# Gate and input of a short convolution: weights stationary in quarters of 256 channels, or activations stationary in halves of 512 channels with a transposed product

## The chip, the cores and the metric

The kernel runs on one core of one Trainium2 chip. The metric is the device time in microseconds (us); the median of three runs is given. A core has five engines that run beside each other: TensorE (PE in the profile; its weight loads are PEld), VectorE (DVE), ScalarE (ACT), GpSimd (POOL) and SyncE (SP), which issues most of the loads here.

## The reference

A trunk of two layers (D_MODEL 2048, SEQ 256, float32). Every layer has attention and a short gated convolution side by side, and behind them an MLP:

```python
h = _rmsnorm(x, attn_norm_g[l])
proj = h @ w_in[l]
q, k, v, gate_b, gate_c, conv_in = jnp.split(proj, splits, axis=-1)    # 1024 columns each
...                                # differential attention, 8 heads -> attn (256 x 1024)
conv = gate_b * _short_conv(gate_c * conv_in, conv_w[l])
x = x + jnp.concatenate([attn, conv.astype(attn.dtype)], axis=-1) @ w_out[l]
hm = _rmsnorm(x, mlp_norm_g[l]) @ w_up[l]
x = x + jnp.square(jax.nn.relu(hm)) @ w_down[l]

def _short_conv(u, w):             # causal, depthwise, CONV_K = 3
    S = u.shape[1]
    up = jnp.pad(u, ((0, 0), (CONV_K - 1, 0), (0, 0)))
    return sum(w[i] * up[:, i:i + S] for i in range(CONV_K))
```

## The kernel before

Every float32 operand of a matrix product is split in two parts: `hi`, a ScalarE copy into a shorter format (L341, tile `whi` for weights), and `lo`, the rest, a VectorE subtraction (L342, `wlo`). A product is the sum of three: hi by hi, hi by lo, lo by hi (`TERMS`). TensorE runs in the order in which the program is written. The other engines are ordered by a tile scheduler.

Two things decide that written order. One is the list of weight jobs: loads of weights into `raw` buffers (four), and their splits (three buffers of each part). They are made in the order of the list, three ahead of the use (`take`). The other is background work: generators (attention of a head, normalisation and so on) that are moved on one piece each time the program calls `work.tick()`, with a number of ticks to wait between pieces. So a head's scores (L712 on), its transposes (`ptp`, L747; `atp`, L793) and its products stand between the matmuls of a projection.

The mixer of one layer goes so: q and k by a scheme that replaces eight block products by seven (`BySeven`); v in two halves of 512 columns by `linear` (L441 to L461: activations are stationary, the weights move as 512 columns, and the result lies by token); then **the stretch that the change rewrites**, with attention in the background; then **the stage of the gate columns**; then the right half of W_out, and the MLP.

The stretch that is rewritten has four quarters of 256 channels. Each has gate_C (`gc`) and conv_in (`ci`), made by `linear_t` (L463 to L488): here 128x128 blocks of weights are stationary and the activations move, hi and lo parts together as 512 columns for `whi`, the hi part alone as 256 columns for `wlo` (both L481). The result lies by channel and has two halves that `joined` adds (ScalarE copy, L493, and VectorE sum, L495: tiles `gc03l`, `gc03w` and the like, the first figure the layer and the second the quarter). The input h is not normalised yet in these products. The factor 1/rms of each token is brought in as a row over all partitions (`norm.bc`): its square multiplies `gc` on GpSimd, and the row itself multiplies the convolved product on GpSimd. The product u = ci * gc is on VectorE, tap 2 of the convolution on ScalarE and taps 1 and 0 on VectorE (L815), all in SBUF.

The stage of the gate columns (`left`) takes its steps from a list, `LEFT`. A step makes a column of 128 gate_B channels (`gb`, by `column_part`, L433, with the same 512 and 256 columns), multiplies it with the convolved product `cv` (`gate`, L824 to L828), or runs products of the seven-product scheme (`po`, L941) on weight splits `w7b`, `w7t`, `w7x` (L880, L916 to L921). `banks` opens the PSUM accumulators of these products. PSUM has two double tiles for accumulators (`mm2`), three single banks used in turn (`bank`) and one for attention (`av`).

Of the kernel before, what the change touches and what calls it, by code (L numbers as in the profile page):

```python
# [133 lines left out]
def trunk(ctx: ExitStack, tc: tile.TileContext, x, w_in, w_out, conv_w, q_norm_g, k_norm_g,  # L134
# [191 lines left out]
    class Weights:  # L326
# [94 lines left out]

        def turned(self, w, col):
            for i in range(D // P // 4):
                self.plain(w, 4 * P * i, col, 4)

    def column_part(acc, acts, weights):
# [13 lines left out]

    def linear(name, acts, weights):  # L441

        acc = mm.tile([P, NT, CH], F32, tag="mm2", name=name)
        nk = len(acts) * KG
        for kp in range(nk // 2):
            hi, lo = weights.take()
            for j in range(2):
                k = kp * 2 + j
                a = acts[k // KG]
                while not a.ready:  # L450
                    work.tick()
                steps = [(t, pa, pw) for t in range(NT) for pa, pw in TERMS]
                if weights.ramp and weights.used == 1 and j == 0:
                    steps = [(t, pa, pw) for pa, pw in ((0, 0), (1, 0), (0, 1)) for t in range(NT)]
                for t, pa, pw in steps:
                    nc.tensor.matmul(  # L456
                        acc[:, t], a.ap[:, pa, k % KG, t * P:(t + 1) * P], (hi, lo)[pw][:, j],
                        start=(k == 0 and (pa, pw) == (0, 0)),
                        stop=(k == nk - 1 and (pa, pw) == TERMS[-1]))
                work.tick()  # L460
        return acc  # L461

    def linear_t(name, acts, weights):  # L463

        acc = mm.tile([P, 2, 2, S], F32, tag="mm2", name=name)
        nk = len(acts) * KG
        for k0 in range(0, nk, 8):  # L470

            tiles = [weights.take() for _ in range(2)]
            for part in range(2):
                for k in range(k0, k0 + 8):
                    a = acts[k // KG]
                    while not a.ready:
                        work.tick()
                    wt = tiles[(k - k0) // 4][part]
                    for f in range(2):
                        fs = slice(f * P, (f + 1) * P)  # L480
                        nc.tensor.matmul(  # L481
                            acc[:, f, 0] if part else acc[:, f], wt[:, k % 4, fs],
                            a.ap[:, 0, k % KG] if part else a.ap[:, :, k % KG],
                            start=(part == 0 and k == 0), stop=(part == 1 and k == nk - 1),
                            skip_group_check=True)
                    if k % 4 == 3 or (part == 0 and k % 2 == 0):
                        work.tick()
        return acc  # L488

    def joined(acc, name):  # L490

        low = nat.tile([P, 2, S], F32, tag="wide", name=f"{name}l")
        nc.scalar.activation(low, acc[:, :, 1], AF.Copy)  # L493
        whole = nat.tile([P, 2, S], F32, tag="wide", name=f"{name}w")
        nc.vector.tensor_add(whole, acc[:, :, 0], low)  # L495
        return whole

# [8 lines left out]
    class Norm:  # L506
# [71 lines left out]
        def factors(self):  # L578
# [25 lines left out]
            while held:  # L604
# [3 lines left out]
                             start=True, stop=True)  # L608
            self.across = small.tile([P, 2, S], F32, tag="rowb", name="rowb", bufs=1)
            nc.vector.tensor_copy(self.across[:, 0], tp[:, :S])  # L610
            nc.gpsimd.tensor_tensor(self.across[:, 1], self.across[:, 0], self.across[:, 0],
                                    op=ALU.mult)

        def bc(self, power):

            return self.across[:, power - 1].unsqueeze(1).to_broadcast([P, 2, S])

# [74 lines left out]
    def attention(l, qT, kT, kL, v, h0, dst, bias, tmp, pace, sums_of):  # L692
# [4 lines left out]
        OFF = (0, P)  # L697
        r0 = small.tile([P, 4, NT], F32, tag="r0", name=f"r0_{h0}", bufs=2)
        ss = small.tile([P, 4, NT], F32, tag="ams", name=f"ams{h0}", bufs=2)
        ao = tmp.tile([P, NT, CH], F32, tag="ao", name=f"ao{h0}", bufs=1)  # L700

        def unit(i):
# [28 lines left out]
            for t in range(NT):  # L731
                for m in range(2):
                    e = s[:, m, OFF[t]:OFF[t] + (t + 1) * P]
                    nc.scalar.activation(e, e, AF.Exp, bias=nm[:, t, m:m + 1],
                                         accum_out=su[:, t, m:m + 1])
            rc = small.tile([P, NT, 2], F32, tag="rc", name=f"rc{h}")
            nc.vector.reciprocal(rc, su)
            nc.vector.tensor_copy(r0[:, i], rc[:, :, 0])
            c = small.tile([P, NT], F32, tag="c", name=f"c{h}", bufs=3)
            p = s[:, 0]  # L740
            for t in range(NT):
                w = slice(OFF[t], OFF[t] + (t + 1) * P)
                nc.vector.scalar_tensor_tensor(c[:, t:t + 1], su[:, t, 0:1], rc[:, t, 1:2],
                                               nlam[:, l:l + 1], op0=ALU.mult, op1=ALU.mult)
                nc.vector.scalar_tensor_tensor(p[:, w], s[:, 1, w], c[:, t:t + 1], s[:, 0, w],
# [27 lines left out]
            flat = ss.rearrange("p i t -> p (i t)")  # L773
            rflat = r0.rearrange("p i t -> p (i t)")
            for _ in range(2):
# [32 lines left out]

    def conv(l, q, u, cv, norm):

        for i in range(2):
            k = q * 2 + i
            nc.scalar.activation(cv[:, k], u[:, i], AF.Copy, scale=tap(l, 2, k))
            for back in (1, 2):
                nc.vector.scalar_tensor_tensor(  # L815
                    cv[:, k, back:], u[:, i, :S - back], tap(l, 2 - back, k),
                    cv[:, k, back:], op0=ALU.mult, op1=ALU.add)
        pair = cv[:, q * 2:q * 2 + 2]
        nc.gpsimd.tensor_tensor(pair, pair, norm.bc(1), op=ALU.mult)

# [15 lines left out]
    class BySeven:  # L836
# [160 lines left out]

        def left(self, acts, cv):

# [174 lines left out]
    def mixer(l, norm, loads):  # L1174

        with ExitStack() as scope:
# [66 lines left out]
            cv = bpool.tile([P, AW // P, S], F32, tag="b", name=f"cv{l}")  # L1243
            for q in range(AW // WC):
# [9 lines left out]
            by_seven.left(hT, cv)  # L1254
            mnorm = Norm(1, l)
# [497 lines left out]
```

## Time and profile before

| | |
|---|---|
| time, median of three runs | 2112.55 us (2112.5 to 2112.66) |
| span of the profiled execution (its own time is given by this span alone) | 2110.7 us |
| median less span | 1.85 us |
| granted TensorE clock | 1.000 |
| TensorE busy (of which it loads weights) | 2105.2 us, 100% (1799.0 us, 85%) |
| VectorE, ScalarE, GpSimd busy | 1834.6 us 87%, 1407.5 us 67%, 189.4 us 9% |
| moved by DMA | 476.01 MB, mean 226 GB/s |

Busy times are sums of one engine's instructions; engines overlap, so they don't add up to the span. A row of the timeline has the start in us from the span's start, the duration of the run of like instructions, engine, line, operation, and out<-in with the tile names (buffer numbers left out), shape and count. Matmuls are pipelined: each lasts longer than the distance to the next one's start, so distances between starts are what adds up. In the table of windows each row is a stretch A:B, its length, then the busy time and count of TensorE, TensorE's weight loads, VectorE, ScalarE and GpSimd, the clock, the share of DMA and its GB/s; with a line named, the times are those of that line's instructions alone. In the timeline, a bracket at a row's end is idle time of the engine ahead of it and what ended it.

### The profile page before, as it was taken

What the parts mean: (1) busy time and instruction counts of PE and PEld (TensorE: products, weight loads), DVE (VectorE), ACT (ScalarE), POOL (GpSimd) and SP (SyncE); (2) the same over time, 40 slices, a digit from 0 to 9 for tenths busy, and PEclk for the clock granted to TensorE, in tenths of its full rate; (3) what the DMA queues carried; (4) which work ended last, traced back from release to release, by engine and by line L of the source; (5) the groups of instructions that cost most, each with busy time, mean ns of one, the idle gap of its engine ahead of it and who ended that gap; (6) DMA issues with size and microseconds to landing.
All of it is one profiled execution on the core that took longest, in us unless ns stands there. A gap on an engine that the chain in (4) does not pass through costs nothing.

```text
span 2110.7 us, 29252 instructions
## 1 busy us (share of the span) xinstructions
PE 2105.2 (100%) x10809; PEld 1799.0 (85%) x10809; DVE 1834.6 (87%) x2525; ACT 1407.5 (67%) x1823; POOL 189.4 (9%) x226
## 2 busy tenths in 40 slices
PE   9999999999999999999999999999999999999999
PEld 7888888888888888888888888888888888888887
DVE  7888788898888888799888887988988888888998
ACT  6777566676776766666566775657676677675664
POOL 2211120000000000011101121000000000000110
PEclk9999999999999999999999999999999999999999
DMA  7655575887777777789566456668777777777993
GB/s 265 205 154 167 171 216 182 289 259 229 230 238 229 231 232 230 251 291 310 171 220 188 152 170 185 195 193 290 255 238 229 229 230 238 230 229 260 315 309 113
DMA packets 312607, 476.01 MB, mean 226 GB/s; under 512 B 12723, under 2 KB 209669, under 8 KB 312464
## 3 DMA queue, kind: packets, MB, share of 16 engines
q1 hardware_dynamic: 284752, 406.76, 60.7%
q0 software_dynamic: 27520, 67.24, 10.1%
q8 instruction: 85, 1.39, 0.3%
q14 instruction: 58, 0.48, 0.1%
q10 hardware_dynamic: 192, 0.15, 0.0%
HBM read 440.52 MB, written 33.58 MB: 225 GB/s over the span
## 4 chain that ended last, share of the span: by engine, by line
PE 98%; DMA 1%; POOL 1%; DVE 1%; issue 0%; ACT 0%; ACTq 0%; DVEq 0%
PE upc L1427 31%; PE pr L1470 14%; PE dn L1551 8%; PE gc L481 4%; PE ci L481 4%; PE gb L433 4%; PE v L456 3%; PE q L958 3%; PE o L958 3%; PE k L958 3%; PE dn L1470 3%; PE po L941 2%; PE dn L1645 2%; PE pr1r L1470 2%; PE pr0r L1470 2%; PE po L958 2%
## 5 line engine op out<-in xcount | busy, mean ns | idle before, releaser
L1427 PE MATMUL upc<-nT,uhi 128*128 128x512 f32 x1920 | 454.7, 389 | 0.0
L1427 PEld LDWEIGHTS upc<-nT,uhi 128*128 128x128 f32 x1920 | 360.2, 188 | 74.7
L1292 DVE TENSOR_TENSOR ulo<-uraw,uhi 128x1024 fp32r<-128x1024 f32 x256 | 312.3, 1222 | 109.8 <-ACT f L1459 91.5
L341 ACT ACTIVATE whi<-raw 128x1024 fp32r<-128x1024 f32 x232 | 244.7, 1058 | 180.2 <-issue 21.8
L1291 ACT ACTIVATE uhi<-uraw 128x1024 fp32r<-128x1024 f32 x256 | 270.6, 1057 | 135.7 <-PE upc L1427 115.4
L342 DVE TENSOR_TENSOR wlo<-raw,whi 128x1024 fp32r<-128x1024 f32 x232 | 284.3, 1234 | 53.1 <-ACT whi L341 46.9
L1427 PEld LDWEIGHTS upc<-nT,ulo 128*128 128x128 f32 x1920 | 246.2, 191 | 9.4
L1427 PE MATMUL upc<-nT,ulo 128*128 128x256 f32 x1920 | 249.1, 283 | 0.0
L1317 ACT ACTIVATE bh<-draw 128x1536 fp32r<-128x1536 f32 x86 | 128.3, 1492 | 103.7 <-PE pr L1470 82.1
L1318 DVE TENSOR_TENSOR bl<-draw,bh 128x1536 fp32r<-128x1536 f32 x86 | 151.3, 1759 | 11.4 <-ACT bh L1317 10.9
L1551 PE MATMUL dn<-whi,fb 128*128 128x512 f32 x480 | 152.0, 389 | 0.0
L1470 PE MATMUL pr<-bh,f 128*128 128x512 f32 x360 | 121.4, 391 | 0.0
L341 ACT ACTIVATE whi<-uraw 128x1024 fp32r<-128x1024 f32 x60 | 63.7, 1062 | 72.0 <-PE dn L1551 58.5
L1437 ACT ACTIVATE ev<-upc 128x512 f32<-128x512 f32 x120 | 72.0, 600 | 54.0 <-PE upc L1427 54.0
L1317 ACT ACTIVATE t24h<-t 128x1024 fp32r<-128x1024 f32 x86 | 91.4, 1063 | 23.7 <-PE pr L1470 15.9
L1551 PEld LDWEIGHTS dn<-whi,fb 128*128 128x128 f32 x480 | 90.1, 188 | 18.6
L1318 DVE TENSOR_TENSOR t24l<-t,t24h 128x1024 fp32r<-128x1024 f32 x86 | 104.9, 1220 | 0.2
L1330 DVE TENSOR_TENSOR t<-draw 128x1024 f32<-128x1024 f32 x86 | 105.0, 1221 | 0.1
L1318 DVE TENSOR_TENSOR t13l<-t,t13h 128x1024 fp32r<-128x1024 f32 x86 | 104.9, 1220 | 0.0
L1317 ACT ACTIVATE t13h<-t 128x1024 fp32r<-128x1024 f32 x86 | 91.5, 1063 | 8.1 <-DVE t L1330 2.9
L1470 PE MATMUL pr<-t13h,f 128*128 128x512 f32 x240 | 93.8, 391 | 0.0
L1551 PE MATMUL dn<-wlo,fb 128*128 128x512 f32 x240 | 93.4, 389 | 0.0
(528 smaller groups left out, 4383.9 us busy)
## 6 DMA issues: line engine op xcount, KB each, us to landing
uraw<-in_w_up_dram SPq DMA_DIRECT2D x128, 1024.0 KB, 6.3
raw<-in_w_in_dram SPq DMA_DIRECT2D x191, 512.0 KB, 4.2
draw<-in_w_down_dram SPq DMA_DIRECT2D x180, 512.0 KB, 5.3
raw<-in_w_out_dram SPq DMA_DIRECT2D x64, 512.0 KB, 4.5
uraw<-in_w_down_dram SPq DMA_DIRECT2D x60, 512.0 KB, 6.8
hid0p<-f POOLq DMA_DIRECT2D x17, 512.0 KB, 3.5
fb<-hid0p POOLq DMA_DIRECT2D x17, 512.0 KB, 8.0
hid1p<-f POOLq DMA_DIRECT2D x17, 512.0 KB, 3.5
```

The source lines that it names most:

```text
L341: pair = (nc.scalar.activation(hi, raw, AF.Copy), nc.vector.tensor_sub(lo, raw, hi.bitcast(F32)))
L342: nc.vector.tensor_sub(lo, raw, hi.bitcast(F32)))
L481: nc.tensor.matmul(acc[:, f, 0] if part else acc[:, f], wt[:, k % 4, fs], a.ap[:, 0, k % KG] if part else a.ap[:, :, k % KG], start=(part ...
L958: nc.tensor.matmul(accs[t], a.ap[:, pa, k % KG, t * P:(t + 1) * P], (hi, lo)[pw][:, j], start=(j == 0 and (pa, pw) == (0, 0) and (n, t) in ...
L1291: pair = (nc.scalar.activation(hi, src, AF.Copy), nc.vector.tensor_sub(lo, src, hi.bitcast(F32)))
L1292: nc.vector.tensor_sub(lo, src, hi.bitcast(F32)))
L1317: keep(nc.scalar.activation(hi, src, AF.Copy))
L1318: keep(nc.vector.tensor_sub(lo, src, hi.bitcast(F32)))
L1330: keep(nc.vector.tensor_sub(t[:, 0:2], raw[:, 0::2], raw[:, 1::-1]))
L1427: nc.tensor.matmul(acc[:, 0] if part else acc, wt[part][:, k], a.ap[:, 0, k % KG] if part else a.ap[:, :, k % KG], start=(part == 0 and kh ...
L1470: nc.tensor.matmul(prods[n], f[:, pa, a], b[pw], start=(start and m == 0), stop=(stop and m == 2))
L1551: nc.tensor.matmul(prods[p], f[:, pa, 2 * k + t], b[pw][:, n], start=(p in starts and k == 0 and m == 0), stop=(stop and k == 1 and m == 2))
```

## The change

gate_C and conv_in are made in two halves of 512 channels by `linear`, as v is. Their weights are loaded as 128x2x512 instead of 128x4x256, 32 loads a layer as before. The results lie by token, so the square of the token's factor is now a scalar of a partition (`norm.r2`): ScalarE multiplies `gc` with it on its way out of PSUM, and VectorE multiplies `ci` out of PSUM with that into `u`. TensorE transposes `u` in blocks of 128x128 into a PSUM bank (`utp`, four to a bank), and the taps read PSUM. The factor's row is applied by VectorE instead of GpSimd. The convolution is a background generator, started four ticks after its half's product, with two groups of channels (`q`) and three ticks between. `banks` opens no accumulator before both halves are through. With `fine`, `linear` ticks once more, after its first token tile. In attention, the softmax sums' reciprocals are kept in one tile (`rcs`) instead of being copied, and the factor `c` of both token tiles is one small instruction instead of two.

```diff
-    def linear(name, acts, weights):
+    def linear(name, acts, weights, fine=False):
...
+                    if fine and (t, pa, pw) == (0, *TERMS[-1]):
+                        work.tick()
                 work.tick()
         return acc
-    def linear_t(name, acts, weights):
...
-    def joined(acc, name):
...
+            self.r2 = small.tile([P, NT], F32, tag="rowf3", name="rowf3", bufs=2)
+            nc.gpsimd.tensor_tensor(self.r2, r, r, op=ALU.mult)
...
-            rc = small.tile([P, NT, 2], F32, tag="rc", name=f"rc{h}")
+            rc = rcs[:, i]
             nc.vector.reciprocal(rc, su)
-            nc.vector.tensor_copy(r0[:, i], rc[:, :, 0])
...
+            nc.vector.scalar_tensor_tensor(c, su[:, :, 0], nlam[:, l:l + 1], rc[:, :, 1],
+                                           op0=ALU.mult, op1=ALU.mult)
...
-    def conv(l, q, u, cv, norm):
-
-        for i in range(2):
-            k = q * 2 + i
-            nc.scalar.activation(cv[:, k], u[:, i], AF.Copy, scale=tap(l, 2, k))
+    def conv(l, half, u, cv, norm, made):
+
+        for q in range(2):
+            tp = bank(f"utp{half}{q}").rearrange("p (k s) -> p k s", k=2)
+            for i in range(2):
+                for t in range(NT):
+                    c = (2 * q + i) * P
+                    nc.tensor.transpose(tp[:, i, t * P:(t + 1) * P], u[:, t, c:c + P], ident)
+            k0 = half * KG + 2 * q
+            for i in range(2):
+                nc.scalar.activation(cv[:, k0 + i], tp[:, i], AF.Copy, scale=tap(l, 2, k0 + i))
             for back in (1, 2):
-                nc.vector.scalar_tensor_tensor(
-                    cv[:, k, back:], u[:, i, :S - back], tap(l, 2 - back, k),
-                    cv[:, k, back:], op0=ALU.mult, op1=ALU.add)
-        pair = cv[:, q * 2:q * 2 + 2]
-        nc.gpsimd.tensor_tensor(pair, pair, norm.bc(1), op=ALU.mult)
+                for i in range(2):
+                    nc.vector.scalar_tensor_tensor(
+                        cv[:, k0 + i, back:], tp[:, i, :S - back], tap(l, 2 - back, k0 + i),
+                        cv[:, k0 + i, back:], op0=ALU.mult, op1=ALU.add)
+            pair = cv[:, k0:k0 + 2]
+            nc.vector.tensor_mul(pair, pair, norm.across.unsqueeze(1).to_broadcast([P, 2, S]))
+            if q == 0:
+                yield 3
+        made.append(half)
...
             def banks():
+                while len(made) < 2:
+                    work.tick()
...
-                    weights.turned(w_in[l], part * AW + q * WC)
+                    weights.straight(w_in[l], 0, D // P, part * AW + half * CH)
...
-            for q in range(AW // WC):
-                acc = linear_t(f"gc{l}{q}", hT, weights)
-                u = joined(acc, f"gc{l}{q}")
-                nc.gpsimd.tensor_tensor(u, u, norm.bc(2), op=ALU.mult)
-                acc = linear_t(f"ci{l}{q}", hT, weights)
-                i = joined(acc, f"ci{l}{q}")
-                nc.vector.tensor_mul(u, i, u)
-                conv(l, q, u, cv, norm)
+            made = []
+            us = biasp.tile([P, 2, NT, CH], F32, tag="bias", name=f"u{l}")
+            for half in range(2):
+                acc = linear(f"gc{l}{half}", hT, weights, True)
+                u = us[:, half]
+                for t in range(NT):
+                    nc.scalar.activation(u[:, t], acc[:, t], AF.Copy, scale=norm.r2[:, t:t + 1])
+                acc = linear(f"ci{l}{half}", hT, weights, True)
+                for t in range(NT):
+                    nc.vector.tensor_mul(u[:, t], acc[:, t], u[:, t])
+                work.start(conv(l, half, u, cv, norm, made), 4)
```

The change moves instructions at the end of the stretch and in the first gate columns. The first place is TensorE from the last matmuls of `ci` to the end of the first gate column `gb`, in layer 0; the number behind a name is the scheduler's. Before:

```order
L481 MATMUL ci_2577<-nT_2_282,whi 128x512 x8
L481 MATMUL ci_2577<-nT_3_340,whi 128x512 x8
L481 MATMUL ci_2577<-nT_2_282,wlo 128x256 x8
L481 MATMUL ci_2577<-nT_3_340,wlo 128x256 x8
L433 MATMUL gb_2716<-nT_0_167,whi 128x512 x4
L433 MATMUL gb_2716<-nT_1_229,whi 128x512 x4
L433 MATMUL gb_2716<-nT_2_282,whi 128x512 x4
L433 MATMUL gb_2716<-nT_3_340,whi 128x512 x4
L433 MATMUL gb_2716<-nT_0_167,wlo 128x256 x4
```

The same place with the change:

```order
L452 MATMUL ci_2341<-wlo,nT_3_340 128x512
L452 MATMUL ci_2341<-whi,nT_3_340 128x512
L429 MATMUL gb_2526<-nT_0_167,whi 128x512 x4
L429 MATMUL gb_2526<-nT_1_229,whi 128x512 x4
L429 MATMUL gb_2526<-nT_2_282,whi 128x512 x4
L429 MATMUL gb_2526<-nT_3_340,whi 128x512 x4
L774 MATMUL utp_2557<-ident,u_1586 128x128 x4
L429 MATMUL gb_2526<-nT_0_167,wlo 128x256 x4
L429 MATMUL gb_2526<-nT_1_229,wlo 128x256 x4
L429 MATMUL gb_2526<-nT_2_282,wlo 128x256 x4
L774 MATMUL utp_2581<-ident,u_1586 128x128 x4
L429 MATMUL gb_2526<-nT_3_340,wlo 128x256 x4
```

The last half's eight transposes now stand inside the first gate column, the first four behind its 16 matmuls on `whi`.

The second place is VectorE where that half's product is made, ahead of the first gate columns (`sv` and `sf` are sums and parts of the seven-product scheme). Before, the last row is the last quarter's join:

```order
L342 TENSOR_TENSOR wlo<-raw,whi 128x1024
L880 TENSOR_TENSOR w7b<-raw,w7b 128x1024
L916 TENSOR_TENSOR w7t<-raw 128x512
L917 TENSOR_TENSOR w7t<-raw 128x512
L863 TENSOR_TENSOR sf<-sv_2664,sf 128x512
L880 TENSOR_TENSOR wlo<-raw,whi 128x512
L863 TENSOR_TENSOR sf<-sv_2675,sf 128x512
L495 TENSOR_TENSOR ci03w<-ci_2577,ci03l 128x512
```

The same place with the change:

```order
L342 TENSOR_TENSOR wlo<-raw,whi 128x1024
L884 TENSOR_TENSOR w7t<-raw 128x512
L829 TENSOR_TENSOR sv_2494<-ay_0_2449,sv_2494 128x128
L885 TENSOR_TENSOR w7t<-raw 128x512
L831 TENSOR_TENSOR sf<-sv_2481,sf 128x512
L1223 TENSOR_TENSOR u_1586<-ci_2341,u_1586 128x512 x2
L848 TENSOR_TENSOR w7b<-raw,w7b 128x1024
```

The two products `u` stand behind three operations of 512 columns and a small sum, and ahead of the split `w7b`.

The third place is VectorE in the first gate columns, around the second split `w7x`. Before:

```order
L825 TENSOR_TENSOR y_2763<-gb_2842 128x256
L916 TENSOR_TENSOR w7t<-raw 128x512
L917 TENSOR_TENSOR w7t<-raw 128x512
L880 TENSOR_TENSOR w7b<-raw,w7b 128x1024
L880 TENSOR_TENSOR wlo<-raw,whi 128x512
L826 TENSOR_TENSOR y_2763<-y_2763,cv_1596 128x256
L921 TENSOR_TENSOR w7t<-w7t,raw 128x512
L880 TENSOR_TENSOR w7x<-w7t,w7x 128x1024
L342 TENSOR_TENSOR wlo<-raw,whi 128x1024
```

The same place with the change:

```order
L793 TENSOR_TENSOR y_2597<-gb_2676 128x256
L848 TENSOR_TENSOR wlo<-raw,whi 128x512
L884 TENSOR_TENSOR w7t<-raw 128x512
L885 TENSOR_TENSOR w7t<-raw 128x512
L784 TENSOR_TENSOR cv_1585<-cv_1585,rowb 128x512
L828 TENSOR_TENSOR sv_2684<-y_2597 128x128
L797 TENSOR_TENSOR cat_2602<-y_2597,cat_2602 128x256
L848 TENSOR_TENSOR w7b<-raw,w7b 128x1024
L794 TENSOR_TENSOR y_2597<-y_2597,cv_1585 128x256
L889 TENSOR_TENSOR w7t<-w7t,raw 128x512
L342 TENSOR_TENSOR wlo<-raw,whi 128x1024
L848 TENSOR_TENSOR w7x<-w7t,w7x 128x1024
```

The scale product `cv` (L784) now stands here, and the split of a later weight (L342) moved from behind `w7x` to ahead of it.

More of the change, by code (lines that the diff above doesn't have):

```diff
@@ L459, in linear @@
                         stop=(k == nk - 1 and (pa, pw) == TERMS[-1]))
+                    if fine and (t, pa, pw) == (0, *TERMS[-1]):
+                        work.tick()
                 work.tick()
         return acc
-    def linear_t(name, acts, weights):
[L468 to L488, printed above, removed]
-    def joined(acc, name):
[L492 to L496, printed above, removed]
     def rstd_of(ss, n, name, shape):
@@ L608, in factors @@
                              start=True, stop=True)
[L609 to L616, printed above, removed]
+            self.across = small.tile([P, S], F32, tag="rowb", name="rowb", bufs=1)
+            nc.vector.tensor_copy(self.across, tp[:, :S])
     HALF = (slice(0, DK), slice(DK, P))
@@ L697, in attention @@
         OFF = (0, P)
-        r0 = small.tile([P, 4, NT], F32, tag="r0", name=f"r0_{h0}", bufs=2)
+        rcs = small.tile([P, 4, NT, 2], F32, tag="r0", name=f"r0_{h0}", bufs=2)
         ss = small.tile([P, 4, NT], F32, tag="ams", name=f"ams{h0}", bufs=2)
@@ L1243, in mixer @@
             cv = bpool.tile([P, AW // P, S], F32, tag="b", name=f"cv{l}")
[L1244 to L1254 removed]
+            made = []
+            us = biasp.tile([P, 2, NT, CH], F32, tag="bias", name=f"u{l}")
+            for half in range(2):
+                acc = linear(f"gc{l}{half}", hT, weights, True)
[6 more added lines that the diff above has]
+                work.start(conv(l, half, u, cv, norm, made), 4)
+            by_seven.left(hT, cv, made)
             mnorm = Norm(1, l)
```

9 lines of the change are left out of this document (2 added, 7 removed).

## The prediction

> **What bounds the kernel now.** I read the page first: its span, its engine line and the line that follows the last chain of work back.
>
> ```profile
> span 2110.7 us, 29252 instructions
> PE 2105.2 (100%) x10809; PEld 1799.0 (85%) x10809; DVE 1834.6 (87%) x2525; ACT 1407.5 (67%) x1823; POOL 189.4 (9%) x226
> PE 98%; DMA 1%; POOL 1%; DVE 1%; issue 0%; ACT 0%; ACTq 0%; DVEq 0%
> ```
>
> TensorE is busy throughout and the chain is 98% TensorE. So the time can fall only where TensorE gets less to do, and it rises by every transpose that is added and by every wait that is new. GpSimd, busy 9%, costs TensorE nothing here, and the large products that leave it buy no time by themselves. The median of the three runs (2112.55 us) stands 1.85 us over the span of the one profiled execution; I carry these 1.85 us unchanged. A difference under 0.2% (4.2 us) I call no change: that is about what a measurement of this kernel can tell.
>
> Next I read the stretch that is rewritten, between the last v matmul and the first gate column, and in it the timeline of TensorE. The two rows are the stretch in layer 0 and in layer 1, counted for the matmuls of L481 alone; the number after the window is its length.
>
> ```profile
> 151.23:251.82 100.59, 93.54 (x512) 77.47 (x511) 1.00 0.55 168
> 1200.46:1301.05 100.59, 93.54 (x512) 77.45 (x511) 1.00 0.55 168
> ```
>
> ```profile
> 228.65 3.82 PE L481 MATMUL gc<-nT,whi 128*128 128x512 f32 x16
> 232.30 2.08 PE L481 MATMUL gc<-nT,wlo 128*128 128x256 f32 x16
> 234.21 3.82 PE L481 MATMUL gc<-nT,whi 128*128 128x512 f32 x16
> 237.87 2.08 PE L481 MATMUL gc<-nT,wlo 128*128 128x256 f32 x16
> 239.78 3.82 PE L481 MATMUL ci<-nT,whi 128*128 128x512 f32 x16
> 243.44 0.60 PE L793 MATMUL atp<-ident,an 128*128 128x128 f32 x4
> 243.79 2.15 PE L481 MATMUL ci<-nT,wlo 128*128 128x256 f32 x16
> 245.78 0.60 PE L793 MATMUL atp<-ident,an 128*128 128x128 f32 x4
> 246.14 3.93 PE L481 MATMUL ci<-nT,whi 128*128 128x512 f32 x16
> 249.91 2.08 PE L481 MATMUL ci<-nT,wlo 128*128 128x256 f32 x16
> ```
>
> Matmuls overlap, so I go by starts. 16 matmuls of 512 columns take 232.30 - 228.65 = 3.65 us (228 ns each) and 16 of 256 take 1.91 us (119.4 ns each). A group of four transposes takes 0.35 us, and the run behind it is longer: 1.99 instead of 1.91 us, and 3.77 instead of 3.65 us. One group therefore costs 0.35 + 0.10 = 0.45 us.
>
> **The change part by part.** *Matmuls.* Each layer has 512 of them in L481, 256 by 512 columns and 256 by 256. They become 384 by 512: the same columns, a quarter fewer instructions. The chain prices the old kind, and two rows of `linear` in the v stage the new one, since the changed code calls that function:
>
> ```profile
> 228.81 11.13 PE gc L481 x64
> 1121.36 5.50 PE v L456 x24
> 1104.68 8.45 PE v L456 x36
> ```
>
> ```profile
> 72.24 0.62 PE L456 MATMUL v<-whi,nT 128*128 128x512 f32 x2
> ...
> 77.00 0.39 PE L456 MATMUL v<-whi,nT 128*128 128x512 f32 x1
> ```
>
> Old: 11.13 / 32 = 347.8 ns a pair, 256 pairs 89.0 us a layer. New, undisturbed: between 72.24 and 77.00 stand 21 matmuls, 226.7 ns each, and 384 of them are 87.05 us, 2.0 us less. With the second row (229 ns) it is 1.0 us less, with the third (235 ns, where splits are short) 1.1 us more. Over two layers that is -4.0 to +2.2 us. I take -3.0, near the undisturbed value, because the weights are split at the same rate as in v and ScalarE and VectorE have less to do in most of the stretch.
>
> Here a rule speaks against the change. The Trainium skill ("TensorE: Matmul & The Clock Gate", section "Back-to-back issue gap") puts a warm matmul at its columns by the clock plus about 2.5 ns. By that, 128 instructions fewer a layer would save only 0.64 us in all, an estimate. This trace disagrees: twice 119.4 less 228 is a fixed part of 11 ns.
>
> *Transposes.* The product lies by token and is turned: 16 transposes a layer, in four groups of four. 8 x 0.45 = +3.6 us, all on TensorE, where nothing hides them.
>
> *VectorE behind the change.* The half of the channels that is finished last has its product, taps and scale fall into the stage of the gate columns (T0 = 251.82, L433). There VectorE has nothing to spare:
>
> ```profile
> 252.00:258.00 6.00, 6.00 (x35) 5.26 (x35) 6.00 (x10) 4.31 (x6) 0.00 (x0) 1.00 0.41 121
> 258.00:264.00 6.00, 6.00 (x30) 4.98 (x29) 6.00 (x8) 3.37 (x6) 0.00 (x0) 1.00 0.61 157
> 264.00:270.00 6.00, 6.00 (x35) 5.25 (x34) 6.00 (x13) 3.51 (x5) 1.90 (x1) 1.00 0.91 294
> 270.00:276.00 6.00, 6.00 (x35) 5.30 (x34) 6.00 (x10) 4.27 (x6) 6.00 (x1) 1.00 0.45 132
> 292.00:300.00 8.00, 8.00 (x45) 6.92 (x44) 6.35 (x9) 4.16 (x7) 0.00 (x0) 1.00 0.85 267
> ```
>
> The fourth column of times is VectorE: full until 276, first slack after 292. What TensorE needs from it most narrowly is the second split w7x of the seven-product scheme. Rows of VectorE, then of TensorE:
>
> ```profile
> 251.12 1.23 DVE L342 TENSOR_TENSOR wlo<-raw,whi 128x1024 fp32r<-128x1024 f32 x1 [0.85 <-ACT w7b L879]
> 252.26 1.22 DVE L880 TENSOR_TENSOR w7b<-raw,w7b 128x1024 fp32r<-128x1024 f32 x1
> ...
> 256.40 0.69 DVE L495 TENSOR_TENSOR ci03w<-ci,ci03l 128x512 f32<-128x512 f32 x1
> 257.00 0.69 DVE L921 TENSOR_TENSOR w7t<-w7t,raw 128x512 f32<-128x512 f32 x1
> ...
> 263.68 0.88 DVE L815 SCALAR_TENSOR_TENSOR cv<-gc03w,gains,cv 128x255 f32<-128x255 f32 x2
> 264.47 0.42 DVE L826 TENSOR_TENSOR y<-y,cv 128x256 f32<-128x256 f32 x1
> ...
> 272.62 1.23 DVE L880 TENSOR_TENSOR w7x<-w7t,w7x 128x1024 fp32r<-128x1024 f32 x1
> 273.75 1.23 DVE L342 TENSOR_TENSOR wlo<-raw,whi 128x1024 fp32r<-128x1024 f32 x1
> ```
>
> ```profile
> 251.82 3.82 PE L433 MATMUL gb<-nT,whi 128*128 128x512 f32 x16
> ...
> 275.35 0.84 PE L941 MATMUL po<-w7x,sf 128*128 128x512 f32 x3
> ```
>
> By starts, a split of 1024 takes 1.14 us (251.12 to 252.26), an operation of 512 takes 0.60, two taps 0.79. From 251.12 to 273.75 VectorE works 22.63 us without a gap. By the new order the same stretch, from that split to the end of this w7x, gains two u products (1.20), four taps (1.58), two scale products (1.20), one weight split that now stands ahead of w7x (1.14) and a small sum (0.2), and loses ci03w and gc03w (1.20): 26.75 us. It can start at most the 0.85 us earlier that VectorE waited at 251.12, so w7x ends between T0 + 25.2 and T0 + 26.05. TensorE's second matmul on it needs it at 275.35 + 0.23, which is T0 + 23.76, and two transpose groups later now, T0 + 24.66. So TensorE waits 0.5 to 1.4 us there in each layer; I take 1.0, together +2.0 us. The bounds are 0 (no wait, if the new operations run shorter or spread) and 2.8. After it the splits have room: VectorE's slack at 292 returns the rest.
>
> *Waits that I price at nothing.* The transposes of the last half wait for u. TensorE reaches them 16 matmuls into the column, T0 + 3.65. VectorE has four operations and a sum ahead (1.14 + 3 x 0.60 + 0.2), then u (1.20): 4.34 us from between T0 - 1.55 and T0 - 0.70, so T0 + 2.8 to T0 + 3.65, just in time. Behind waiting transposes would stand all of TensorE; each 0.1 us later costs 0.1 us. In the first half VectorE stands less full and TensorE has a head's scores between. The transposes take two of three PSUM banks in turn, so po number 5 takes over the bank of the first gate column; TensorE is there nine matmuls (2.0 us) after the column, and ScalarE empties it ahead of that, as it does now: in 0.60 us, and done at 258.19 where the column's matmuls end at 257.4:
>
> ```profile
> 257.59 0.60 ACT L824 ACTIVATE gb<-gb 128x512 f32<-128x512 f32 x1
> ```
>
> The loads of SP are as many and as large, in rows twice as long. The shorter softmax factor, the small r2 product on GpSimd and the smaller row tile touch no wait of TensorE.
>
> *Sum.* -3.0 + 3.6 + 2.0 = +2.6 us: span 2113.3, time 2115.15; I give 2115.1.
>
> **The rivals.**
>
> *Plain exchange (0.24).* If w7x is in time, the sum is -3.0 + 3.6 = +0.6 us: 2113.1. For it: the schedule has many splits whose rows leave TensorE 2 us of room. Against it: VectorE's full windows.
>
> *VectorE falls behind (0.26), slower.* The same queue in the stage of the gate columns, but more than one split late: the u product held back by a sum that waits for its load, then w7b, w7x and the following round. Its price is one for one on TensorE. With 2.5 us a layer: -3.0 + 3.6 + 5.0 = +5.6, time 2118.15. It decides over 0.2% from 1.8 us of waiting a layer, since 4.2 - 0.6 = 3.6 for two. For it: w7b of the second round has by the same count no room left either. Against it: only w7x comes out late by the rows.
>
> *A matmul has no fixed price that can be saved (0.04), slower.* Then the exchange gains nothing: +3.6 + 2.0 = +5.6, time 2118.15. Against it stand the rows of v at 226.7 ns. By the 2.5 ns of the Trainium skill's page "TensorE: Matmul & The Clock Gate" ("Back-to-back issue gap") it would be 2117.5, an estimate.
>
> *Less disturbance (0.06), faster.* The stretch has 3.65 and 3.77 us where 16 x 226.7 is 3.63; if all such surplus goes, some 0.7 us a layer, without a VectorE wait: -4.0 - 1.4 + 3.6 = -1.8, time 2110.7. That is still within 0.2%; I leave 0.04 for a gain above that, from something the rows do not show.
>
> That the change does not do what it says is excluded by the order: transposes and 512-column matmuls stand there, and the GpSimd products are gone.
>
> **How the numbers follow.** Forecast 0.40, time 2115.1, on the slow side but inside 0.2%. No change: forecast 0.40, plain exchange 0.24, 0.02 of the fast case, 0.66. Slower: 0.26 + 0.04 = 0.30. Faster: 0.04. The range goes from the plain exchange with the full matmul gain (-4.0 + 3.6 = -0.4, 2112.15), a little below, to the case of VectorE (2118.15), a little above: 2111.5 to 2118.5.
>
> **What would show it.** Rewritten stretch: matmuls of gc and ci at 227 to 229 ns by starts, 16 transposes a layer at 0.35 us a group, window about 100.4 us. In the gate stage: an idle row of TensorE at po on w7x or a longer start-to-start there, released by VectorE, 0.5 to 1.4 us. Wrong would be: no such wait; a wait of the transposes for u; waits of the matmuls in gc for splits; or a change of time in stages that the diff does not touch.

## The result, and the profile after

| | before | after |
|---|---|---|
| median | 2112.62 us (13 runs) | 2117.62 us (13 runs) |
| ratio to before | | 1.0023 (1.0015 to 1.0031) |
| span of the profiled execution | 2110.7 us | 2115.8 us |

The change costs 5.0 us, a little over the 0.2% (4.2 us) that counted as a change; the interval of the ratio reaches below that. The forecast was 2115.1 us with a range to 2118.5, and "no change", its likeliest verdict at 0.66, is not what came.

The page of the changed kernel, its span, its engines and the line on the last chain:

```profile
span 2115.8 us, 28707 instructions
PE 2107.3 (100%) x10585; PEld 1788.6 (85%) x10585; DVE 1821.6 (86%) x2485; ACT 1403.0 (66%) x1815; POOL 146.3 (7%) x212
PE 97%; DVE 2%; DMA 1%; issue 0%; POOL 0%; ACT 0%; DVEq 0%; ACTq 0%; POOLq 0%
```

TensorE still fills the span, but VectorE now has 2% of the chain. The table of waits says where (engine, line, what it waited for; us in total, times, longest). It has three rows that before does not have:

```profile
PE po L909 <- DVE w7x L848: 1.3, 2, 0.7
PE atp L751 <- DVE an L741: 1.2, 2, 0.6
...
PE po1r L909 <- DVE w7y L848: 0.5, 1, 0.5
```

The windows of the rewritten stretch, layer 0 and layer 1 (length, then TensorE, its weight loads, VectorE, ScalarE, GpSimd), and TensorE's rows at a small wait for a split, at the transposes of the last half and at the three waits of the table:

```profile
151.14:252.28 101.14, 100.46 (x488) 83.37 (x488) 72.52 (x143) 68.00 (x135) 5.50 (x10) 1.00 0.55 167
1203.29:1304.33 101.04, 100.36 (x488) 83.37 (x488) 72.51 (x143) 67.98 (x135) 5.50 (x10) 1.00 0.55 167
```

```profile
160.81 0.48 PE L452 MATMUL gc<-whi,nT 128*128 128x512 f32 x1
161.36 0.50 PE L452 MATMUL gc<-wlo,nT 128*128 128x512 f32 x1
...
176.25 0.39 PE L452 MATMUL gc<-whi,nT 128*128 128x512 f32 x1
177.26 0.63 PE L751 MATMUL atp<-ident,an 128*128 128x128 f32 x4 [0.62 <-DVE an L741]
...
255.97 0.60 PE L774 MATMUL utp<-ident,u 128*128 128x128 f32 x4
256.32 1.68 PE L429 MATMUL gb<-nT,wlo 128*128 128x256 f32 x12
...
276.71 0.39 PE L909 MATMUL po<-w7x,sf 128*128 128x512 f32 x1
277.77 0.73 PE L909 MATMUL po<-w7x,sf 128*128 128x512 f32 x2 [0.68 <-DVE w7x L848]
...
1089.10 0.39 PE L909 MATMUL po1r<-w7y,sf 128*128 128x512 f32 x1
1089.97 0.74 PE L909 MATMUL po1r<-w7y,sf 128*128 128x512 f32 x2 [0.48 <-DVE w7y L848]
```

A matmul of 512 columns is followed 0.23 us later when nothing waits. By starts the three waits therefore cost 1.01 - 0.23 = 0.78 us (attention's transposes `atp`, in each layer), 1.06 - 0.23 = 0.83 us (`w7x`, in each layer) and 0.87 - 0.23 = 0.64 us (`w7y`, once, where layer 1 begins). Together that is 3.9 of the 5.1 us between the spans of the two profiled executions. The transposes of `u` do not wait. One wait is too short for the table: the first matmul behind an interruption, at 160.81, lasts 0.55 us to the next start, because VectorE's split `wlo` for the next one ends only at 161.31. The same stands in layer 1; against the 0.31 us of other such matmuls it costs some 0.24 us a layer.

VectorE's rows around the late split, in the stage of the gate columns:

```profile
254.07 1.28 DVE L1223 TENSOR_TENSOR u<-ci,u 128x512 f32<-128x512 f32 x2
...
275.37 1.21 DVE L342 TENSOR_TENSOR wlo<-raw,whi 128x1024 fp32r<-128x1024 f32 x1
276.50 1.22 DVE L848 TENSOR_TENSOR w7x<-w7t,w7x 128x1024 fp32r<-128x1024 f32 x1
```

The product `u` is through at 255.35 (254.07 + 1.28), 0.6 us ahead of its transposes. `w7x` ends at 277.7, which is 25.4 us behind the start of the first gate column (252.3), and TensorE stands still for it.

### The profile page after: what moved, and what is told of

Its sections match the earlier page's. It is cut to its first block, busy times and chain, and to the rows that moved or that the text cites. A ratio compares the mean times of both kernels' runs of the same rounds, so it can differ in the third digit from the quotient of the medians.

```text
span 2115.8 us, 28707 instructions
## 1 busy us (share of the span) xinstructions
PE 2107.3 (100%) x10585; PEld 1788.6 (85%) x10585; DVE 1821.6 (86%) x2485; ACT 1403.0 (66%) x1815; POOL 146.3 (7%) x212
## 4 chain that ended last, share of the span: by engine, by line
PE 97%; DVE 2%; DMA 1%; issue 0%; POOL 0%; ACT 0%; DVEq 0%; ACTq 0%; POOLq 0%
PE upc L1400 31%; PE pr L1443 14%; PE dn L1524 8%; PE v L452 4%; PE ci L452 4%; PE gb L429 4%; PE gc L452 4%; PE q L926 3%; PE o L926 3%; PE k L926 3%; PE dn L1443 3%; PE po L909 2%; PE dn L1618 2%; PE pr1r L1443 2%; PE pr0r L1443 2%; PE po L926 2%
## 5 line engine op out<-in xcount | busy, mean ns | idle before, releaser
L342 DVE TENSOR_TENSOR wlo<-raw,whi 128x1024 fp32r<-128x1024 f32 x232 | 282.5, 1220 | 86.0 <-ACT whi L341 81.9
```

What stands on the lines that cost most here:

```text
L342: nc.vector.tensor_sub(lo, raw, hi.bitcast(F32)))
```

## The experiments

Ratios are to the kernel before, in the same session on the same chip; the last column is the median less 2117.62 us, the changed kernel's in its own session. The medians of before differ by up to 0.14 us between the sessions, so the last column is not good to a tenth.

| kernel | median us | against before (95%) | against the changed kernel |
|---|---|---|---|
| e1, attention part alone, on before | 2126.31 | 1.0065 (1.0053 to 1.0078) | |
| e5, e1 and 64 bytes of room | 2112.44 | 0.9999 (0.9991 to 1.0008) | |
| e12, before and 64 bytes of room | 2124.87 | 1.0060 (1.0047 to 1.0072) | |
| e2, scale products on GpSimd | 2116.27 | 1.0018 (1.0009 to 1.0027) | -1.35 us |
| e4, `av` one tick earlier | 2117.28 | 1.0023 (1.0014 to 1.0032) | -0.34 us |
| e7, r2 on VectorE | 2117.53 | 1.0023 (1.0014 to 1.0032) | -0.09 us |
| e8, three mendings | 2114.25 | 1.0009 (1.0000 to 1.0017) | -3.37 us |
| e3, no transposes | 2124.04 | 1.0056 (1.0043 to 1.0069) | +6.42 us |
| e9, transposes twice | 2119.30 | 1.0034 (1.0021 to 1.0046) | +1.68 us |
| e10, e8 with transposes twice | 2116.92 | 1.0021 (1.0012 to 1.0030) | -0.70 us |
| e11, e8 with groups of eight | 2115.29 | 1.0013 (1.0004 to 1.0022) | -2.33 us |
| e6, matmuls of 256 columns | 2124.96 | 1.0061 (1.0048 to 1.0073) | +7.34 us |

**e1, the attention part alone.** The kernel before with these edits:

```diff
-            rc = small.tile([P, NT, 2], F32, tag="rc", name=f"rc{h}")
+            rc = rcs[:, i]
             nc.vector.reciprocal(rc, su)
-            nc.vector.tensor_copy(r0[:, i], rc[:, :, 0])
...
+            nc.vector.scalar_tensor_tensor(c, su[:, :, 0], nlam[:, l:l + 1], rc[:, :, 1],
+                                           op0=ALU.mult, op1=ALU.mult)
```

> The kernel before with the attention part of the change alone (reciprocals kept in one tile, one small instruction for c instead of two, no copy). Theory 1 (the new wait of TensorE at atp comes from where the attention products av land among the matmuls, not from the softmax factor): no wait at atp, time within 0.5 us of before. Theory 2 (the shorter softmax factor lets the scheduler put the exponentials ahead of the copy ao on ScalarE, so an comes late): a wait at atp of about 0.6 us a layer, time before + 1.3 us.

It came out 13.8 us slower, which no theory had, and with no wait at `atp`. The loss was spread over all stages. The buffers gave the next question: without the tile `rc`, and with `rcs` in place of the smaller `r0`, the pool of small tiles is 64 bytes a partition shorter, and the pools placed behind it begin 192 bytes off a multiple of 256. Before begins them at byte 108032 of a partition and the changed kernel at 107008, both multiples of 256, because there the smaller `rowb` and the new `rowf3` make up the difference.

**e5, the same with 64 bytes of room.**

```diff
     small = ctx.enter_context(tc.tile_pool(name="small", bufs=4))
+    small.tile([P, 16], F32, tag="room", name="room", bufs=1)
```

> The kernel with the attention part alone, which came out 13.8 us slower with TensorE slower in every stage (its 512-column matmuls 1.6 to 3.3 ns each, the MLP included), and 64 bytes a partition added to the pool of small tiles. In that kernel the pool is 64 bytes a partition shorter than before, and all pools placed behind it (splits, raw weights, activations) begin 192 bytes off a multiple of 256, where before and in the changed kernel they begin at a multiple of 256. Theory 1 (the place of the buffers in SBUF makes the matmuls slower, the attention edits are neutral): time within 0.7 us of before, matmuls in the MLP back at 227.7 ns. Theory 2 (the order of instructions or the edits themselves make it slow): still about 2126 us.

**e12, the kernel before with the room alone.**

> The kernel before with 64 bytes a partition added to its pool of small tiles and nothing else, so that all pools behind it begin 64 bytes off a multiple of 256. Theory 1 (the place of the buffers makes the matmuls slower): 512-column matmuls of the MLP at 229 ns or more instead of 227.7, time 8 to 14 us over before. Theory 2 (what made the attention part slow was another thing that the 64 bytes took away by chance): within 0.5 us of before.

Theory 1 held in both: e5 is back at the time of before, e12 is 12.4 us over it. One row of the chain shows it as an example: 48 matmuls of 512 columns of W_out's products (`po`), in before, e1, e5 and e12 in this order:

```profile
325.88 10.88 PE po L958 x48
```

```profile
327.21 11.00 PE po L957 x48
```

```profile
325.67 10.88 PE po L958 x48
```

```profile
327.39 11.20 PE po L959 x48
```

With the pools at a multiple of 256 a matmul of this row takes 226.7 ns, at 192 bytes off 229 ns, at 64 bytes off 233 ns. That the place of the buffers does it is shown from both sides: 64 bytes took the loss away from e1 and gave it to before. Other distances, 128 bytes among them, were not run. The attention edits themselves are neutral (e5).

**e2, the scale products on GpSimd.**

```diff
-            nc.vector.tensor_mul(pair, pair, norm.across.unsqueeze(1).to_broadcast([P, 2, S]))
+            nc.gpsimd.tensor_tensor(pair, pair, norm.across.unsqueeze(1).to_broadcast([P, 2, S]),
+                                    op=ALU.mult)
```

> The changed kernel with the scale products of the convolved half (128x512, four a layer) back on GpSimd. Theory 1 (VectorE's queue in the first gate columns makes w7x late; each wait is time lost): VectorE has two products of 0.60 us less ahead of the second w7x, the wait of 0.68 us there goes, and the time falls by 1.5 to 2.0 us for two layers. Theory 2 (TensorE's work alone sets the time, what is waited for at w7x is paid elsewhere when the wait goes): time stays within 0.5 us of the changed kernel. Theory 3 (a large GpSimd product slows VectorE beside it): VectorE's splits beside those products take longer than 1.23 us, the wait stays or moves, time between the changed kernel and 1 us over it.

The wait at `w7x` is gone and the time fell by 1.35 us, a little less than theory 1's 1.5: VectorE's queue was the cause. Theory 3 has its part too. GpSimd's rows and VectorE's beside them:

```profile
266.71 3.23 POOL L784 TENSOR_TENSOR cv<-cv,rowb 128x512 f32<-128x512 f32 x2 [33.80 <-DVE cv L780]
```

```profile
266.12 1.22 DVE L849 TENSOR_TENSOR w7y<-w7t,w7y 128x1024 fp32r<-128x1024 f32 x1
...
268.71 2.31 DVE L342 TENSOR_TENSOR wlo<-raw,whi 128x1024 fp32r<-128x1024 f32 x1
```

A split that takes 1.22 us took 2.31 us beside the product. Here nobody waited for it. The Trainium skill ("SBUF — State Buffer", section "SBUF: two separate sides") names the port that VectorE and GpSimd share as one of two places of contention; the row agrees.

**e4, `av` one tick earlier**, and `atp` one tick later behind it, so that `atp` keeps its place.

```diff
-            yield 8 if h == 3 else 4 * pace
+            yield 7 if h == 3 else 4 * pace
...
-            yield 12 * pace
+            yield 13 if h0 == 0 else 12 * pace
```

> The changed kernel with the products av of the fourth head one tick earlier and its atp one tick later behind them, so that atp stands where it stood and av 0.7 us earlier; by the order ScalarE then copies ao ahead of the next head's four exponentials. Theory 1 (av came 0.5 us later than before, the exponentials went ahead of ao, and an came 1.3 us later): no wait at atp, an ready before TensorE comes, time -1.2 us to -1.4 us for two layers. Theory 2 (an is late for VectorE's splits ahead of it or for the chain of GpSimd): the wait stays at 0.6 us a layer, no change of time.

The cause is theory 1's, the price is not: -0.34 us where -1.2 to -1.4 was expected. The products `av` start at 167.06 in before and at 167.58 in the changed kernel:

```profile
167.06 0.28 PE L761 MATMUL av<-v,pT 128*128 128x256 f32 x1
```

```profile
167.58 0.28 PE L719 MATMUL av<-v,pT 128*128 128x256 f32 x1
```

ScalarE in before does the copy `ao` first, and in the changed kernel the next head's four exponentials (`s`) ahead of it:

```profile
167.92 0.37 ACT L766 ACTIVATE ao<-av 128x256 f32<-128x256 f32 x1
168.19 0.39 ACT L734 ACTIVATE s<-s,nm 128x128 f32<-128x128 f32 x1
```

```profile
168.74 0.39 ACT L693 ACTIVATE s<-s,nm 128x128 f32<-128x128 f32 x1
...
170.50 0.36 ACT L724 ACTIVATE ao<-av 128x256 f32<-128x256 f32 x1
```

With `av` a tick earlier the copy goes first, and `atp` does not wait. But another wait comes 2.5 us later: the scores `sc` wait for `ay`, the operation with which ScalarE reads `atp` out of its PSUM bank. ScalarE and then TensorE in e4:

```profile
167.94 0.39 ACT L724 ACTIVATE ao<-av 128x256 f32<-128x256 f32 x1 [0.73 <-PE av L721]
168.35 0.40 ACT L693 ACTIVATE s<-s,nm 128x128 f32<-128x128 f32 x1
```

```profile
179.06 0.33 PE L679 MATMUL sc<-kT,qT 128*128 128x128 f32 x2
179.72 0.50 PE L676 MATMUL sc<-kL,both 128*128 128x512 f32 x1 [0.32 <-ACT ay L754]
```

**e7, r2 on VectorE.**

```diff
-            nc.gpsimd.tensor_tensor(self.r2, r, r, op=ALU.mult)
+            nc.vector.tensor_tensor(self.r2, r, r, op=ALU.mult)
```

> The changed kernel with the small product r2 (128x2) on VectorE instead of GpSimd; TensorE's order is the same. Theory 1 (r2 stands on GpSimd ahead of the bias loads of layer 1, sends them 1 us later, they collide with a weight load, and w7y at the start of layer 1 comes 0.5 us late): the bias loads start 0.8 to 1.0 us earlier relative to TensorE, no wait at po1r, time -0.5 us. Theory 2 (the weight load is late for the drift of TensorE against the loads): wait and time stay.

GpSimd where layer 1 begins, in the changed kernel and in e7:

```profile
1065.41 0.71 POOL L466 TENSOR_TENSOR row_r<-row_e,mhalf 128x2 f32<-128x2 f32 x1
1066.20 0.20 POOL L550 TENSOR_TENSOR rowf<-row_r 128x2 f32<-128x2 f32 x1
1068.66 1.89 POOL L290 DMA_DIRECT2D rev<-by_dist_d  x2 [2.26 <-PE q L926]
```

```profile
1066.64 0.71 POOL L466 TENSOR_TENSOR row_r<-row_e,mhalf 128x2 f32<-128x2 f32 x1
1069.15 1.87 POOL L290 DMA_DIRECT2D rev<-by_dist_d  x2 [1.80 <-DMA raw<-in_w_in_dram]
```

The bias loads `rev` start 3.25 us behind `row_r` in the one and 2.51 us in the other, and e7 has no wait at `po1r`. The traces of the other runs agree: with r2 on GpSimd the distance is 3.25 us and TensorE loses 0.3 to 0.8 us at `po1r` by starts (the changed kernel, e2, e3, e4, e6, e9); with r2 on VectorE it is 2.4 to 2.5 us and nothing is lost (e7, e8, e10, e11). But e12, which has no r2 and the short distance, loses 0.5 us there too. So r2 sets when the bias loads go out, and moving it took the wait away, but other things can make the same wait. That the bias loads collide with a weight load, as theory 1 has it, was not shown. The time shows no gain: the profiled run of e7 lost 1.5 us in its first ten, and its median is not to be told from the changed kernel's.

**e8, the three mendings together** (e2, e7, and `av` and `atp` one tick earlier).

> The changed kernel with three mendings together: scale products on GpSimd, r2 on VectorE, av and atp of the fourth head one tick earlier. Theory 1 (each wait was time and they are separate): 2117.6 - 1.35 (scale products, measured) - 0.5 (r2) - 1.2 (atp, if no other wait takes its place) = 2114.5; what is then left over before is the transposes less the matmuls. With 0.3 us a layer of waiting for a PSUM bank, as in the run with av alone: 2115.2. Theory 2 (waits move on from one to the next): not below 2116.

2114.25 us: 0.25 us under theory 1. The three waits are gone; of TensorE's waits in these stages only the small one for a split in `gc` is left (160.85 to 161.40 here). The windows of the stretch, as above:

```profile
151.23:251.52 100.29, 100.23 (x488) 83.46 (x487) 71.95 (x141) 67.88 (x135) 8.57 (x12) 1.00 0.56 168
1200.76:1301.05 100.29, 100.23 (x488) 83.47 (x487) 71.96 (x141) 67.88 (x135) 8.58 (x12) 1.00 0.56 168
```

With two groups of transposes in it (2 x 0.35 us) the stretch is 0.30 us shorter than before. The exchange of matmuls is thus worth 1.0 us a layer, the small wait included. The other two groups cost more than what is left: the first gate column lasts 6.41 us here (251.53 to 257.94) and 5.57 us in before (251.82 to 257.39), 0.84 us more. This is the price of the change without the three waits: 1.1 us by these windows, 0.9 us by the two spans (2111.6 and 2110.7), 1.7 us by the medians, or nothing at the lower end of the interval.

**e3, without the transposes.**

```diff
-            tp = bank(f"utp{half}{q}").rearrange("p (k s) -> p k s", k=2)
-            for i in range(2):
-                for t in range(NT):
...
+            tp = u[:, q].rearrange("p (k s) -> p k s", k=2)
```

> The changed kernel without its 32 transposes: the taps read u in SBUF as it lies, so what is convolved is not the reference's (the turn of u is left out). Theory 1 (a group of four transposes costs 0.35 us and what it interrupts about 0.05 us): 8 groups less, -3.0 to -3.3 us, and the VectorE waits stay as they are or grow by what TensorE arrives earlier there: w7x waits 0.4 us a layer more at most, so -2.2 us at the least. Theory 2 (the matmuls take up what the transposes leave, no time is won): within 0.5 us of the changed kernel.

Both theories missed. With some 3 us less to do, the kernel became 6.4 us slower. It has waits at `w7y` that the changed kernel doesn't have:

```profile
PE po L905 <- DVE w7y L844: 4.9, 2, 2.5
PE po L905 <- ACT w7y L843: 2.3, 2, 1.1
```

ScalarE in e3 ahead of that:

```profile
264.57 1.06 ACT L341 ACTIVATE whi<-raw 128x1024 fp32r<-128x1024 f32 x1 [3.12 <-DMA raw<-in_w_in_dram]
265.78 0.60 ACT L788 ACTIVATE gb<-gb 128x512 f32<-128x512 f32 x1 [0.15 <-PE gb L429]
266.48 1.06 ACT L843 ACTIVATE w7y<-w7t 128x1024 fp32r<-128x1024 f32 x1
```

The scheduler put ScalarE's half of `w7y` behind the copy of a weight that had not been loaded (in the changed kernel `w7y` comes first, at 262.21, and that copy at 264.38), and VectorE's half followed later still. Two taps take 0.88 us here and 0.86 us from PSUM, so it is the order and not slower taps; why the scheduler chose it was not separated.

The waits are not all of the loss. Behind them the granted TensorE clock (the third number from the end) is not 1.00:

```profile
270.00:276.00 6.00, 5.46 (x17) 4.34 (x18) 6.00 (x13) 2.97 (x5) 0.00 (x0) 0.72 0.33 94
```

From 271.7 on it was 0.50 for 3.4 us, and again at the same place in layer 1; 16 matmuls of 512 columns took 5.19 us there instead of 3.62. By starts the waits cost 4.0 us a layer and the clock some 1.7 us, 11.5 us in all. Against that stand the transposes (2.7 to 3.1 us) and the waits at `w7x` (1.7 us), which e3 does not have: 6.7 to 7.1 us, where 6.42 was measured.

**e9 and e10, every transpose twice**, in the changed kernel and in e8:

```diff
+                    for _ in range(2):
                         nc.tensor.transpose(tp[:, i, t * P:(t + 1) * P], u[:, t, c:c + P], ident)
```

> The changed kernel with every transpose of u made twice into the same place (32 more, four at a time behind the first four). Theory 1 (88.6 ns each on TensorE, but where TensorE waits for w7x behind them, the second four fill the wait): 16 in the rewritten stretch +1.42 us, 16 in the gate column +1.42 us of which the waits at w7x (0.9 us a layer) take back 1.4 us; in all +1.4 to +1.7 us. Theory 2 (work and waits add): +2.8 us.

> The kernel with the three mendings, in which TensorE waits nowhere in these stages, with every transpose made twice. Theory 1: no wait is there to be filled, 32 x 88.6 ns = +2.8 us against the mended kernel. Theory 2 (transposes hide beside something): under 1.5 us.

+1.68 and +2.67 us, as theory 1 has it in both. In e9 the table of waits has no `w7x` any more: the second transposes stand where TensorE would wait. Where the three waits are gone (e10), 32 transposes cost 83 ns each. So a wait and new work on the waiting engine do not add up.

**e11, groups of eight.**

```diff
+        tps = []
...
+            tps.append(tp)
+        for q in range(2):
+            tp = tps[q]
...
-            if q == 0:
-                yield 3
...
+        yield 1
```

> The kernel with the three mendings, with the eight transposes of a half in one group instead of two of four. Theory 1 (each interruption of a run of matmuls costs TensorE 0.05 to 0.1 us beside the transposes): four interruptions less, -0.2 to -0.4 us against the mended kernel, if the second bank and VectorE's taps make no new wait. Theory 2 (interruptions cost nothing of their own): no change, or slower by a new wait for u.

Slower than e8 by 1.04 us, through a new wait. TensorE, VectorE and GpSimd there:

```profile
266.91 0.40 PE L913 MATMUL po<-w7y,sf 128*128 128x512 f32 x1
267.86 0.74 PE L913 MATMUL po<-w7y,sf 128*128 128x512 f32 x2 [0.55 <-DVE w7y L852]
```

```profile
265.97 1.83 DVE L852 TENSOR_TENSOR w7y<-w7t,w7y 128x1024 fp32r<-128x1024 f32 x1
```

```profile
265.42 3.53 POOL L788 TENSOR_TENSOR cv<-cv,rowb 128x512 f32<-128x512 f32 x2 [33.45 <-DVE cv L784]
```

This time it was `w7y` that lay beside the GpSimd product and took 1.83 instead of 1.22 us. What the saved interruptions are worth stays open.

**e6, matmuls of 256 columns.** The two halves of a bank are opened one after the other here, which changes what is summed; only its time is read.

```diff
+                    for part in range(2 if fine else 1):
+                        cs = slice(part * CH // 2, (part + 1) * CH // 2) if fine else slice(0, CH)
                         nc.tensor.matmul(
-                        acc[:, t], a.ap[:, pa, k % KG, t * P:(t + 1) * P], (hi, lo)[pw][:, j],
+                            acc[:, t, cs], a.ap[:, pa, k % KG, t * P:(t + 1) * P],
+                            (hi, lo)[pw][:, j, cs],
```

> The changed kernel with each 512-column matmul of gc and ci written as two of 256 columns with the same stationary activations: 768 instructions more over two layers, the same columns. Theory 1 (a matmul has a fixed price, 2 x 119.5 - 226.7 = 12.3 ns): +9.4 us at the most, less where VectorE's waits take up to 2 us of it. Theory 2 (no fixed price that counts, instructions are nearly free): under 2 us.

+7.34 us for 768 instructions: 9.6 ns each. Theory 1 holds, its 12.3 ns were the upper end. At this price the 128 matmuls that the change saves in a layer are worth 1.2 us; less the small wait for a split that is about the 1.0 us of e8. By the 2.5 ns that the Trainium skill ("TensorE: Matmul & The Clock Gate", section "Back-to-back issue gap") adds to the columns of an isolated matmul it would have been 1.9 us, an estimate. This is a stream of matmuls, each with a weight load of its own, and there the measurement decides.

## Why the prediction was right or wrong

Range and direction held; the verdict held to be the likeliest did not. The forecast is 2.5 us short, and that the time still lies in the range is in part luck: the upper end was taken from a rival, more than one late split in VectorE's queue, that did not happen. The sum was short in three terms (matmuls, `atp`, r2) and a little long in two (transposes, `w7x`).

- **Matmuls:** forecast -3.0 us, measured -2.0 (e8, 1.0 us a layer). That a matmul has a price of its own was right (e6). The step that failed is the choice "near the undisturbed value". Attention interrupts the stretch some 20 times a layer, as before, and by starts the first new matmul behind an interruption takes some 290 ns instead of 227; the old ones take 272 ns instead of 228 (512 columns) and 192 ns instead of 119.5 (256). In all the 384 new ones took 89.5 us a layer in e8, 233 ns each, where 87.05 was counted undisturbed, and the 512 old ones 90.5 us in before, where 89.0 was counted. So the third row of v (235 ns) was near the price of a new matmul, but the prediction set it against an undisturbed price of the old ones. Its second row, 1.0 us less a layer, gave the right size.
- **Transposes:** forecast +3.6 us, measured 2.7 (e10, which adds no new interruption) to 3.1 (0.35 us for each of four groups in the stretch, where what they disturb is counted with the matmuls, and 0.42 us for each of four in the gate columns).
- **`w7x`:** forecast 1.0 us a layer, end at 25.2 to 26.05 us behind the column's start; measured 0.83 us and 25.4. This step, counted from the order and the durations of before, was right in place and size, and e2 and e9 confirm its cause.
- **The wait for `u`, PSUM banks, loads of SP:** priced at nothing, and nothing was there. `u` was ready 3.0 us behind the column's start, TensorE came at 3.65. Of the signs of being wrong that the prediction named, "waits of the matmuls in gc for splits" is there in small, some 0.24 us a layer.
- **What was missed, `atp`:** 2 x 0.78 us. Waits were looked for only where new operations stand. But the new matmuls also shift where the ticks fall: `av` came half a microsecond later than before, and the scheduler's order on ScalarE turned; with `av` a tick earlier it turned back (e4). The prediction had dismissed this part of attention with "touch no wait of TensorE"; the edits there are indeed neutral (e5), the tick is not (e4).
- **What was missed, r2 on GpSimd:** 0.64 us in that trace, not shown in the time (e7). A product of 0.2 us was priced at nothing. It stands ahead of two DMA issues, and they moved by 0.7 us.

New sum: -2.0 + 3.1 + 1.7 + 1.6 + 0.6 = +5.0, where 5.0 was measured (5.1 by the spans).

Of the rivals, "VectorE falls behind" came nearest to the measured time (2118.15 against 2117.62), but by another mechanism: it wanted 2.5 us a layer at `w7x` and what follows it, where 0.83 was found, and nothing later in that queue was late. "Plain exchange" is nearly what e8 makes of the kernel: forecast 2113.1, measured 2114.25. "No fixed price" fell with e6, "less disturbance" with the waits and with matmuls of 233 ns.

## What to carry to other kernels

Where one engine is busy all the time, price a change by its work on that engine first: here 128 fewer matmuls a layer were worth 1.0 us and 16 transposes more cost 1.5, so that the exchange could not win even without waits. Then look for waits not only at the new instructions but wherever the change shifts the order of others: `av` half a microsecond later cost 1.6 us here, half of what the transposes did, and a small product ahead of a DMA issue moved the loads behind it by more than its own length. Less work for the busy engine is no gain by itself either, if it changes the order of what that engine waits for (e3). And before a change of buffers is judged, compare where the pools begin.

## What the runs showed of the hardware

The place of a buffer in SBUF changes the speed of matmuls: pools at 64 or 192 bytes off a multiple of 256 cost 12.4 and 13.8 us (e12, e1). By starts, `pr` on `whi` and `f` went from 226.5 ns to 230.6 (192) and 233.2 ns (64); both operands of `upc` lie in pools that had not moved, and it still went from 226.7 to 229.3 and 227.8 ns, while `gc` and `upw` stayed as they were. Which accesses collide was not separated.

After TensorE had stood idle twice within some 4 us, for 1.15 and 2.45 us, the granted clock was 0.50 for 3.4 us, in both layers of e3. After single waits of 0.6 to 0.7 us in the changed kernel it stayed at 1.00.
